# One encoder layer with 32 experts: token rows fetched from DRAM by indirect DMA in place of gather products, and 20 weight buffers in place of 16

## Chip, cores and metric

The kernel runs on one core of one Trainium2 chip. The metric is the device time of one execution in microseconds (us); lower is better. Engines are named as in the profile: PE is TensorE (PEld its weight loads), DVE VectorE, ACT ScalarE, POOL GpSimd, SP SyncE. SP, ACT and POOL each have an instruction queue from which they also start DMA transfers, one after another.

## What is computed

One layer on 512 tokens of width 1024, in float32. The attention half (three groups of heads, one input and one output projection, residual) is unchanged. The second half sends every token to 2 of 32 experts and adds the results to the residual:

```python
exp_idx = grp_idx[:, None] * EXPERTS_PER_GROUP + top_idx      # 2 experts per token
...
def expert_block(args):
    xb, e = args
    a = jax.nn.silu(xb @ w1[e]) * (xb @ w3[e])
    return a @ w2[e]
...
y = jnp.zeros((n + 1, d), h.dtype).at[row_tok].add(yb * row_gate[:, None].astype(h.dtype))
```

There are 512 x 2 = 1024 rows of tokens in all, spread over 32 experts. Every expert has w1 and w3 of 1024 x 512 and w2 of 512 x 1024, 6 MiB together. All 192 MiB of expert weights are read once.

## The kernel before

The program is a fixed order of instructions for every engine. It has three stages that matter here.

**Attention and projections** (up to about 364 us). `Group` objects load 1 MiB of w_in each, split it into a high and a low half and multiply; head units run beside them. Towards the end `wo_products` multiplies by w_out.

**Routing** (`route`, about 364 to 396 us). For each of four blocks of 128 tokens the kernel forms the normalised rows, the router's logits, the two experts and each row's place among that expert's rows. The order of its instructions comes from a small planner, `run_tasks`, with a duration for each task. Per block, ACT writes the rows in a rounded form `th` (`high`, L1141) and in full (`full`, L1146, two halves), and POOL subtracts them into the rest `tl` (`low`, L1151), so that `th + tl` is the row. `first_gather` (L1248) starts the gather for the first experts: a product of `th` and `tl` with a 0/1 matrix `G`, which picks tokens and turns them so that features lie on partitions.

**Experts** (from 396 us). Experts are worked in 16 pairs, expert pr and expert pr + 16 in the two halves of the array, 64 rows each. For a pair, `gate_half` and `hidden` multiply by w1 and w3 (`up_half`, L1398, tile h), turn the hidden rows (L1480, tile uTp), and `expert_out` multiplies by w2 (L1496, tile y). `combine` (L1416, L1417, tile c) adds the result to the tokens' rows with a 0/1 matrix `ot`; it is emitted inside the next pair's first product. `gather` (L1387, tile xTp) makes the next rows: two 16-product pieces per pair, each product 256 columns wide, for two pairs of experts at once, so every second pair finds its rows ready. `last_out` is the last pair, with its w2 cut into smaller pieces.

**Weights.** The 192 MiB come in 192 loads of 1 MiB, in the order in which they are used: four for w1, four for w3, four for w2 of each pair. (The last six are cut into smaller transfers.) `load_w` (L918) puts each on SP's queue. Load n goes to the buffer `RING[n % 16]`; a granule is a tile of 128 x 2048 float32, which one load fills. Several granules serve the attention stage first (b, q, h, g, m), others exist only once that stage's memory is free (d, e, j, k, v, w). Before the ninth load the ring is

```python
RING = "b q h h g g m m h h d e j k v w".split()
```

A transfer waits on SP until everything that reads the buffer's old content is done. All transfers behind it on SP's queue wait with it.

Of the kernel before, what the change touches and what calls it, by code (L numbers as in the profile page):

```python
# [23 lines left out]
P = 128  # L24
S = 512
# [10 lines left out]
RING = "b q h h g g m m h h d e j k v w".split()  # L36
# [8 lines left out]
def tile_encoder(ctx: ExitStack, tc, x, mem, g_mix, g_mem, g_ffk, w_in, w_kv, w_out, gains,  # L45
# [5 lines left out]
    gov = drp.tile([S, NE], F32, name="gov")  # L51
    man = ExitStack()
# [7 lines left out]
    BUFS = {"q": 1, "g": 2, "h": 4, "b": 1, "m": 2}  # L60
# [558 lines left out]
    def qk_tile(name, dt=F32):  # L619
        return big.tile([P, 2, S], dt, name=name, tag="qk", bufs=6)  # L620
# [11 lines left out]
    def qk(base, gi, order, rot, dd, key):  # L632
        def post(g, a, p):
            if key not in dd:
                dd[key] = qk_tile("qk")
# [33 lines left out]
    def na_v(n):  # L669
        def post(g, b, p):  # L670
            if "a" not in box_v:
                box_v["a"] = big.tile([P, 4, 512], F32, name="va", tag="va")
            return v_turn(g, b, p, "col", fac[:, 3, 0], box_v["a"][:, :, (2 * n + b) * P:(2 * n + b + 1) * P])
        return Group(w_in, VA + 256 * n, post, dims=True)
# [309 lines left out]
    load_w()  # L984
# [38 lines left out]
    at = small("at", [P, 4, 16])  # L1023
# [11 lines left out]
    def G_tile():  # L1035
        return rk.tile([P, 4, 2, P], F32R, name="G", tag="G")

    th, tl, Gs, first_x = [None] * 4, [None] * 4, [], []
# [48 lines left out]
    def route():  # L1087
# [12 lines left out]
        def rows(a):  # L1100
# [20 lines left out]
            for n in (1, 0):  # L1121
                t = task("P", 0.44, lambda n=n: turn_x(n), x_done.get((a, n)), *pt_free[-NPT:][:1] if len(pt_free) >= NPT else ())
                c = task("A", 0.48, lambda n=n: copy(n), t, rl_done.get(a - 2))
                pt_free.append(c)
                rl = task("P", 0.8, lambda n=n: logits_x(n), c, rl, free_lg.get(a - 2))
# [9 lines left out]
            def high():  # L1135
                if a < 3:
                    th[a], tl[a] = [qk_tile("th", F32R).rearrange("p a b -> p (a b)") for _ in range(2)]
                else:
                    t = big.tile([P, 4, 512], F32R, name="th3", tag="va")
                    th[a], tl[a] = t[:, 0:2].rearrange("p a b -> p (a b)"), t[:, 2:4].rearrange("p a b -> p (a b)")  # L1140
# [3 lines left out]
            def full(n):  # L1144
                st["f", n] = r2.tile([P, 2, 256], F32, name="xr", tag="pr", bufs=NPR).rearrange("p a b -> p (a b)")
                nc.scalar.activation(st["f", n].rearrange("p (k q) -> p q k", k=4),  # L1146
                                     x1[:, a].rearrange("p (q k) -> p q k", k=KT)[:, :, 4 * n:4 * n + 4], AF.Copy, scale=r)

            def low(n):
                c = slice(n * 512, (n + 1) * 512)  # L1150
                nc.gpsimd.tensor_sub(tl[a][:, c], st["f", n], th[a][:, c])  # L1151
            hi_done = task("A", 1.05, high, r_done)
            for n in range(2):
                f_done[a, n] = task("A", 0.62, lambda n=n: full(n), r_done, f_done.get((a - 2, n)))
                f_done[a, n] = task("G", 1.23, lambda n=n: low(n), hi_done, f_done[a, n])
            choose(a, lgt)

        def choose(a, lgt):
# [47 lines left out]
            t = v(0.1, lambda: V.tensor_add(at[:, a], d()[:, 0:16], d()[:, 16:32]), t)  # L1206

            for j in range(2):
                def slots(j=j):
                    if not Gs:  # L1210
                        Gs.append(G_tile())
                    V.tensor_scalar(Gs[0][:, a, j], places_, at[:, a, j:j + 1], None, op0=ALU.is_equal)
                G_last.append(v(0.2, slots, t))
# [25 lines left out]
            free_lg[a] = t[1]  # L1239
# [3 lines left out]
            def first_gather(i):  # L1243
                if a == 0:
                    first_x.append(bank("pj", 2, "xq"))
                for k in (2 * i, 2 * i + 1):
                    for n, t in enumerate((th[a], tl[a])):
                        nc.tensor.matmul(first_x[i][:, (k % 2) * 256:(k % 2) * 256 + 256], t[:, k * P:(k + 1) * P], Gs[0][:, a],  # L1248
                                         start=(a == 0 and k % 2 == 0 and n == 0), stop=(a == 3 and n == 1), skip_group_check=True)
            gt_ = None  # L1250
            for i in range(2):
                gt_ = task("P", 0.43, lambda i=i: first_gather(i), *G_last[-2:], f_done[a, 0], x_got.get((a - 1, i)), last_p[0], gt_)
                x_got[a, i] = gt_
# [9 lines left out]
        for a, n in LISTED:  # L1263
            block[0] = a

            def mm(a=a, n=n):
                wo_products(a, n, (0, 1, 2, 3))
                parts[a, n] = pos[n]
            p = task("P", 2.57, mm, *wop_prev[-2:-1], *last_p)
            last_p[:] = [p]  # L1270
            x_done[a, n] = task("V", 0.6, lambda a=a, n=n: add_x(a, n, parts[a, n]), p)
            wop_prev.append(x_done[a, n])
            sq_done[a, n] = task("A", 0.62, lambda a=a, n=n: square(a, n), x_done[a, n])
# [4 lines left out]
        task("P", 3.0, lambda: None, x_got[3, 1])  # L1278
# [31 lines left out]
    for n in range(2):  # L1310
        for a in range(4):
# [4 lines left out]
            def before():  # L1316
# [4 lines left out]
                if a == 0 and n == 1:  # L1321
                    load_w()
# [13 lines left out]
    load_w(2)  # L1336
# [11 lines left out]
    for tag, n, bufs in (("xT", 2, 6), ("u", 2, 1), ("uT", 2, 1), ("ringw", 8, 1), ("ringv", 8, 1)):  # L1348
        for _ in range(bufs):
            wk_.tile([P, n * 256], F32, name="place", tag=tag, bufs=bufs)  # L1350

    def scale_x(q, k0):
        xT = wk_.tile([P, 2, 2 * P], F32, name="xT", tag="xT", bufs=6)
        V.tensor_tensor(xT, q, gfk[:, 0, k0:k0 + 2].unsqueeze(2).to_broadcast([P, 2, 2 * P]), op=ALU.mult)  # L1354
        return xT

    xT = [scale_x(q.rearrange("p (k s) -> p k s", k=2), 2 * i) for i, q in enumerate(first_x)]
# [17 lines left out]
    def spread(pr):  # L1375

        G = G_tile()
        V.tensor_tensor(G, places_.unsqueeze(1).unsqueeze(1).to_broadcast([P, 4, 2, P]),
                        at[:, :, pr:pr + 2].unsqueeze(3).to_broadcast([P, 4, 2, P]), op=ALU.is_equal)
        return G  # L1380

    def gather(G, k0):
# [6 lines left out]
        return scale_x(q.rearrange("p (k j) s -> p k (j s)", j=2), k0)  # L1389
# [4 lines left out]
    def up_half(pr, w, q, p, between=()):  # L1394
        for k in range(4 * q, 4 * q + 4):
            for h in range(2):
                o = pr % 2 * P + h * 64
                nc.tensor.matmul(p[h * 64:(h + 1) * 64, :], xT[k // 2][:, k % 2, o:o + 64], wt[pr, w, q, h][:, k % 4, :],  # L1398
# [3 lines left out]
            if k % 4 == 1:  # L1402
                while between:
                    between.pop(0)()

    def up(pr, w, between=()):
        p, between = up_tile(w), list(between)
        for q in range(2):
            up_half(pr, w, q, p, between)
# [32 lines left out]
    G = Gs[0]  # L1442
    load_w(2)
    between, nxt = [], []
    p_first = []

    def gate_half(pr):
        nonlocal G, between
        if pr:
            p1 = up(pr, 0, between)  # L1450
        else:
# [4 lines left out]
            xT.extend([gather(G, k0) for k0 in (4, 6)])  # L1456
            up_half(0, 0, 1, p1)
        between = []
        u = wk_.tile([P, F], F32, name="u", tag="u", bufs=1)
        nc.scalar.activation(u, p1, AF.Silu)  # L1460
        if pr % 2 == 0 and pr + 2 < NPAIR:
            G = spread(pr + 2)
        return u

    def hidden(pr, u):

        nonlocal xT, nxt, between
        if pr:
            p3 = up(pr, 1, between)
# [3 lines left out]
        between = []  # L1473
        V.tensor_mul(u, u, p3)  # L1474
        rest = pr // 2 * 2 + 2 < NPAIR
        if rest:
            nxt.append(gather(G, pr % 2 * 4))
# [5 lines left out]
        if rest:  # L1483
            nxt.append(gather(G, pr % 2 * 4 + 2))
        if pr % 2:
            xT, nxt = nxt, []
# [19 lines left out]
    def last_out(pr, uT):  # L1506
# [13 lines left out]
        def gated(c0, n):  # L1520

            yh, yl = [wk_.tile([P, 512], F32R, name="y" + c, tag="xT", bufs=6)[:, 0:n] for c in "hl"]
# [20 lines left out]
        while between:  # L1543
            between.pop(0)()
# [30 lines left out]
    with tc.If(flag > 0):  # L1575
        with tc.tile_pool(name="ov", bufs=1) as ov, tc.tile_pool(name="ovps", bufs=1, space=PS) as ovs:
            with tc.For_i(0, NE) as e:
# [6 lines left out]
                for a in range(4):  # L1584
# [3 lines left out]
                    V.tensor_add(t, th[a], tl[a])  # L1588
# [3 lines left out]
                    for k in range(KT):  # L1592
                        q = ovs.tile([P, P], F32, name="ovq1")
                        nc.tensor.transpose(q, t[:, k * P:(k + 1) * P], ident)
# [89 lines left out]
```

## Time and profile before

| | us |
|---|---|
| median of 3 runs (874.48 to 875.97) | 874.78 |
| the profiled execution | 875.22 |
| its span | 873.4 |
| PE busy | 841.9 (96%) |
| DVE, ACT, POOL busy | 434.0, 267.1, 142.6 |

The profiled execution is 1.8 us longer than its span and 0.4 us longer than the median. The mean granted clock of TensorE is 0.98 of full. Matmuls overlap and their ends are modelled, so a busy share of 100% doesn't by itself say that PE is the limit; how often it waits, and for what, has to be read beside it. The second page section gives each engine's busy tenths in 40 slices, and the bytes moved in each; a slice in which the bytes per second stand at their highest and do not move is one in which the transfers run without a gap.

### The profile page before, as it was taken

How to read it: one execution, taken by the hardware profiler on the slowest of the kernel's cores; microseconds unless marked ns; L12 is line 12 of the kernel's file. 1: busy time of each engine (PE TensorE's matmuls, PEld its weight loads, DVE VectorE, ACT ScalarE, POOL GpSimd, SP SyncE). 2: the span in 40 equal slices, each digit the busy share in tenths (PEclk: the TensorE clock that was granted, in tenths of full speed). 3: DMA queues.
4: the chain of work that ended last, by engine and by line, in shares of the span. 5: the costliest groups of instructions: out<-in, count | busy, mean ns of one | idle time of the engine just before them, and what ended most of it. 6: DMA issues, size and time to landing. Idle time of an engine off the chain costs nothing.

```text
span 873.4 us, 13351 instructions
## 1 busy us (share of the span) xinstructions
PE 841.9 (96%) x5086; PEld 545.1 (62%) x5086; DVE 434.0 (50%) x1208; ACT 267.1 (31%) x776; POOL 142.6 (16%) x141
## 2 busy tenths in 40 slices
PE   7799999999899999989999999999999999999995
PEld 7789889879778767884545454545454545354333
DVE  6787796448759567482413241334133413341323
ACT  5667665665535544570010001000100010000001
POOL 5453222243322324160000000000000000000000
PEclk8999999999999999978999999999999999999998
DMA  9233113122122376848999999999999999999983
GB/s 314 73 97 105 50 51 96 49 74 92 49 78 62 101 216 231 328 146 318 375 421 422 419 421 421 421 421 421 421 421 421 421 421 421 422 421 420 421 298 99
DMA packets 63475, 237.53 MB, mean 272 GB/s; under 512 B 8240, under 2 KB 32816, under 8 KB 39600
## 3 DMA queue, kind: packets, MB, share of 16 engines
q1 hardware_dynamic: 55376, 230.18, 66.7%
q10 hardware_dynamic: 8032, 6.45, 3.0%
q8 instruction: 42, 0.69, 0.3%
q14 instruction: 25, 0.20, 0.1%
HBM read 234.45 MB, written 2.16 MB: 271 GB/s over the span
## 4 chain that ended last, share of the span: by engine, by line
PE 77%; DVE 12%; ACT 3%; DMA 3%; issue 3%; POOL 1%; ACTq 0%; DVEq 0%; SPq 0%; POOLq 0%
PE h L1398 26%; PE y L1496 12%; PE xTp L1387 7%; PE pj L231 4%; PE c L1416 4%; PE pj L232 3%; PE pj L233 3%; PE c L1417 3%; PE pj L241 1%; DMA nab<-in_na_tab_dram 1%; PE pj L243 1%; PE pj L242 1%; PE acc L392 1%; PE lg L348 1%; DVE rw L282 1%
## 5 line engine op out<-in xcount | busy, mean ns | idle before, releaser
L1398 PE MATMUL h<-w,xT 128*64 128x512 f32 x1024 | 227.2, 596 | 0.0
L1398 PEld LDWEIGHTS h<-w,xT 128*64 128x64 f32 x1024 | 72.0, 137 | 141.7 <-issue 139.0
L1496 PE MATMUL y<-w,uT 128*64 128x512 f32 x480 | 106.3, 595 | 0.0
L188 POOL TENSOR_TENSOR wp<-wc,wp 128x512 fp32r<-128x512 f32 x51 | 66.9, 1315 | 129.6 <-ACT wp L187 109.4
L1474 DVE TENSOR_TENSOR u<-u,h 128x512 f32<-128x512 f32 x16 | 11.0, 688 | 150.1 <-PE h L1398 150.1
L231 PE MATMUL pj<-wp,hTh 128*128 128x256 f32 (+1 forms) x268 | 79.3, 296 | 1.9 <-ACT hTh L768 1.0
L1419 DVE TENSOR_TENSOR x<-x,c 128x512 f32<-128x512 f32 x120 | 73.1, 682 | 12.3 <-PE c L1417 12.3
L232 PE MATMUL pj<-wp,hTh 128*128 128x256 f32 (+1 forms) x268 | 76.7, 286 | 1.3 <-POOL wp L188 1.3
L233 PE MATMUL pj<-wp,hTl 128*128 128x256 f32 (+1 forms) x268 | 76.5, 285 | 0.2 <-DVE hTl L771 0.2
L1496 PEld LDWEIGHTS y<-w,uT 128*64 128x64 f32 x480 | 33.2, 137 | 62.5 <-issue 59.4
L1502 DVE SCALAR_TENSOR_TENSOR yl<-y,gate,yh 128x512 fp32r<-128x512 f32 x30 | 22.5, 751 | 94.5 <-ACT yh L1501 94.5
L1387 PEld LDWEIGHTS xTp<-G,th 128*128 128x128 f32 x480 | 59.3, 189 | 12.2 <-issue 12.2
L1387 PE MATMUL xTp<-G,th 128*128 128x256 f32 x480 | 64.9, 287 | 0.0
L1460 ACT ACTIVATE u<-h 128x512 f32<-128x512 f32 x16 | 9.6, 597 | 149.6 <-PE h L1398 149.6
L1501 ACT ACTIVATE yh<-y,gate 128x512 fp32r<-128x512 f32 x30 | 20.6, 687 | 112.6 <-PE y L1496 111.6
L231 PEld LDWEIGHTS pj<-wp,hTh 128*128 128x128 f32 (+1 forms) x268 | 51.6, 192 | 4.9 <-issue 1.4
L232 PEld LDWEIGHTS pj<-wp,hTh 128*128 128x128 f32 (+1 forms) x268 | 51.6, 193 | 1.7 <-POOL wp L188 1.7
L1482 ACT ACTIVATE uT<-uTp 128x512 f32<-128x512 f32 x16 | 9.6, 597 | 139.3 <-PE uTp L1480 139.3
L233 PEld LDWEIGHTS pj<-wp,hTl 128*128 128x128 f32 (+1 forms) x268 | 51.6, 192 | 0.4 <-DVE hTl L771 0.4
L1416 PE MATMUL c<-yh,ot 128*128 128x512 f32 x120 | 48.7, 406 | 0.0
L1417 PE MATMUL c<-yl,ot 128*128 128x512 f32 x120 | 47.0, 392 | 0.0
L1354 DVE TENSOR_TENSOR xT<-xTp,gfk 128x512 f32<-128x512 f32 x30 | 20.8, 692 | 52.5 <-PE xTp L1387 52.5
(315 smaller groups left out, 1481.1 us busy)
## 6 DMA issues: line engine op xcount, KB each, us to landing
w<-in_w_dram SPq DMA_DIRECT2D x188, 1024.0 KB, 13.1
wc<-in_w_in_dram SPq DMA_DIRECT2D x15, 1024.0 KB, 5.5
wo<-in_w_out_dram SPq DMA_DIRECT2D x4, 1024.0 KB, 5.1
w<-in_w_dram SPq DMA_DIRECT2D x6, 512.0 KB, 15.0
wc<-in_w_kv_dram SPq DMA_DIRECT2D x2, 1024.0 KB, 8.3
x<-in_x_dram ACTq DMA_DIRECT2D x4, 512.0 KB, 9.4
nab<-in_na_tab_dram ACTq DMA_DIRECT2D x8, 248.0 KB, 2.8
x_sb<-in_x_dram SPq DMA_DIRECT2D x3, 512.0 KB, 6.2
```

What stands on the lines that cost most here:

```text
L188: (eng or nc.gpsimd).tensor_sub(dst[1], src, dst[0])
L231: nc.tensor.matmul(o, th, self.hi[k], start=(k == 0), stop=False)
L232: nc.tensor.matmul(o, th, self.lo[k], start=False, stop=False)
L233: nc.tensor.matmul(o, tl, self.hi[k], start=False, stop=(k == KT - 1))
L1354: V.tensor_tensor(xT, q, gfk[:, 0, k0:k0 + 2].unsqueeze(2).to_broadcast([P, 2, 2 * P]), op=ALU.mult)
L1387: nc.tensor.matmul(q[:, 2 * (k - k0):2 * (k - k0) + 2, :], t[a][:, k * P:(k + 1) * P], G[:, a], start=(n == 0), stop=(n == 7))
L1398: nc.tensor.matmul(p[h * 64:(h + 1) * 64, :], xT[k // 2][:, k % 2, o:o + 64], wt[pr, w, q, h][:, k % 4, :], start=(k == 0), stop=(k == KT ...
L1416: nc.tensor.matmul(c, ot[:, a], yh, start=True, stop=False)
L1417: nc.tensor.matmul(c, ot[:, a], yl, start=False, stop=True)
L1419: V.tensor_add(sl, sl, c)
L1496: nc.tensor.matmul(y[h * 64:(h + 1) * 64, :], uT[:, f, h * 64:(h + 1) * 64], rows_of(wt[pr, 2, q, h])[:, f % 2, n * 512:(n + 1) * 512], st ...
L1502: V.scalar_tensor_tensor(yl, y, gate[:, pr:pr + 1], yh, op0=ALU.mult, op1=ALU.subtract)
```

## The change

1. Each block's normalised rows are written once in full (`full`), to the granules k0 (blocks 0 and 1) and va (blocks 2 and 3), and stored to a DRAM tensor `xd` by ACT's queue (4 transfers of 512 KiB). The rounded rows, the rest and POOL's subtractions go.
2. The first pair's rows are still made by products, now in float32 from the full rows, 128 columns wide: 16 in `first_gather` for half the features, 16 in `gather_first` for the other half, after the first pair's first two half products.
3. For the 15 other pairs, POOL issues one indirect DMA each: 128 places of one row of 4 KiB, by an index list `where_`; a place without a row has an index out of range and is left alone. PE turns the rows (`turn_rows`, 8 transposes per pair). Two buffers take turns, and a fetch goes out when the buffer's rows have been turned.
4. `combine` of a pair now stands in the next pair's `hidden`, between the transposes and the product with w2.
5. A query tile and its key tile share a granule (k0, k1, k2), and with va these four become weight buffers: the ring has 20. The first load moves behind the last load of w_out; four loads are emitted at once there, four one step later, four more after `route`.

```diff
-RING = "b q h h g g m m h h d e j k v w".split()
+RING = "k2 b q k1 h h g g k0 va m m h h d e j k v w".split()
...
-                nc.scalar.activation(th[a].rearrange("p (k q) -> p q k", k=KT), x1[:, a].rearrange("p (q k) -> p q k", k=KT),
-                                     AF.Copy, scale=r)
...
-                nc.gpsimd.tensor_sub(tl[a][:, c], st["f", n], th[a][:, c])
...
+            def full():
+                if a % 2 == 0:
+                    xr2.append(granule(("k0", "va")[a // 2], "xr"))
+                xr.append(xr2[a // 2][:, 2 * (a % 2):2 * (a % 2) + 2].rearrange("p a b -> p (a b)"))
+                nc.scalar.activation(xr[a], x1[:, a], AF.Copy, scale=r)
+
+            def store():
+                nc.scalar.dma_start(xd[a * P:(a + 1) * P], xr[a])
...
-                if a == 0 and n == 1:
-                    load_w()
+                if a == 2 and n == 1:
+                    load_w(4)
                 if a == 3 and n == 1:
                     load_w(4)
...
     route()
-    load_w(2)
+    load_w(4)
...
+    def rows_load(pr):
+        if pr < NPAIR:
+            nc.gpsimd.indirect_dma_start(out=rows_in[pr % 2], out_offset=None, in_=xd,
+                                         in_offset=bass.IndirectOffsetOnAxis(ap=where_[:, pr:pr + 1], axis=0),
+                                         bounds_check=S - 1, oob_is_err=False)
...
+    def gather_first():
 
         q = trp("xTp")
-        for k in (k0, k0 + 1):
-            for n, (t, a) in enumerate((t, a) for a in range(4) for t in (th, tl)):
-                nc.tensor.matmul(q[:, 2 * (k - k0):2 * (k - k0) + 2, :], t[a][:, k * P:(k + 1) * P], G[:, a],
-                                 start=(n == 0), stop=(n == 7))
...
+        for k in range(4, KT):
+            for a in range(4):
+                nc.tensor.matmul(q[:, k - 4], xr[a][:, k::KT], Gs[0][:, a], start=(k == 4 and a == 0), stop=(a == 3), skip_group_check=True)
+        return scale_x(q, 1)
+
+    def turn_rows(pr):
+        nxt = []
+        for half in range(2):
+            q = trp("xTp")
+            for k in range(4):
+                nc.tensor.transpose(q[:, k], rows_in[pr % 2][:, 4 * half + k::KT], ident)
+            nxt.append(scale_x(q, half))
+        rows_load(pr + 2)
+        return nxt
```

The weight transfers on SP's queue around the ninth one. A name is w, which weight (0 is w1, 1 is w3, 2 is w2), expert, half, a running number; in brackets stand the semaphores that the transfer, or a wait just ahead of it, waits for. Before:

```order
L938 DMA w0_0_1_4481<-in_w1_dram 128x2048 [waits DMAHW5_49,Pool_49]
L938 DMA w0_16_1_4483<-in_w1_dram 128x2048 [waits DMAHW6_49,Pool_49]
L938 DMA w1_0_1_5041<-in_w3_dram 128x2048 [waits DMAHW7_49,DVE_49]
L938 DMA w1_16_1_5043<-in_w3_dram 128x2048 [waits DMAHW0_49]
L940 DMA w2_0_0_5053<-in_w2_dram 128x2048 [waits DMAHW1_49,PE_49]
L940 DMA w2_16_0_5055<-in_w2_dram 128x2048 [waits DMAHW2_49,PE_49]
L940 DMA w2_0_1_5057<-in_w2_dram 128x2048 [waits DMAHW3_49,DVE_49,PE_49]
L940 DMA w2_16_1_5059<-in_w2_dram 128x2048 [waits DMAHW4_49,DVE_49,PE_49]
```

And now:

```order
L946 DMA w0_16_1_4479<-in_w1_dram 128x2048 [waits DMAHW6_49]
L946 DMA w1_0_1_4481<-in_w3_dram 128x2048 [waits DMAHW7_49,Pool_49]
L946 DMA w1_16_1_4483<-in_w3_dram 128x2048 [waits DMAHW0_49,Pool_49]
L948 DMA w2_0_0_4995<-in_w2_dram 128x2048 [waits DMAHW2_49,DMAHW1_49,DMAHW5_49,PE_49,Activation_49]
L948 DMA w2_16_0_4997<-in_w2_dram 128x2048 [waits DMAHW4_49,DMAHW3_49,DMAHW6_49,PE_49,Activation_49]
L948 DMA w2_0_1_4999<-in_w2_dram 128x2048 [waits DMAHW7_49]
L948 DMA w2_16_1_5001<-in_w2_dram 128x2048 [waits DMAHW0_49]
L946 DMA w0_1_0_5011<-in_w1_dram 128x2048
L946 DMA w0_17_0_5013<-in_w1_dram 128x2048
```

The ninth and tenth transfers (w2 of experts 0 and 16, first halves) now go to k0 and va, which hold the full rows of tokens, and wait for ACT, for the stores to xd and for PE's last reading of those rows; the ones after them wait for little of their own.

PE at the end of `hidden` of an early pair, from the last product with w3 to the first with w2. Before (pair 0):

```order
L1398 MATMUL h_5097<-w_16_1_5043,xT 64x512
L1387 MATMUL xTp<-G,th 128x256 x6
L1387 MATMUL xTp<-G,th_4936 128x256 x2
L1387 MATMUL xTp<-G,th 128x256 x6
L1387 MATMUL xTp<-G,th_4936 128x256 x2
L1480 MATMUL uTp<-ident,u 128x128 x4
L1387 MATMUL xTp<-G,th 128x256 x6
L1387 MATMUL xTp<-G,th_4936 128x256 x2
L1387 MATMUL xTp<-G,th 128x256 x6
L1387 MATMUL xTp<-G,th_4936 128x256 x2
L1496 MATMUL y<-w_0_0_5053,uT 64x512
```

And now (pair 1):

```order
L1408 MATMUL h_5235<-w_17_1_5079,xT 64x512
L1397 MATMUL xTp<-ident,rows 128x128 x8
L1480 MATMUL uTp<-ident,u 128x128 x4
L1423 MATMUL c<-yh,ot 128x512
L1424 MATMUL c<-yl,ot 128x512
```

The 32 gather products of a pair became 8 transposes, and the 16 products of `combine` (the last two rows, eight times) stand ahead of y.

## Rows read from the trace of the kernel before

**Rows 1.** page, the span in 40 slices of 21.8 us: PE busy tenths, GB/s moved:

```profile
PE   7799999999899999989999999999999999999995
...
GB/s 314 73 97 105 50 51 96 49 74 92 49 78 62 101 216 231 328 146 318 375 421 422 419 421 421 421 421 421 421 421 421 421 421 421 422 421 420 421 298 99
```

**Rows 2.** busy time by window: PE, PEld, DVE, ACT, POOL, PEclk, DMA share, GB/s:

```profile
385.00:390.00 5.00, 4.49 (x25) 4.28 (x25) 3.82 (x26) 4.20 (x6) 2.68 (x7) 0.50 0.00 2
390.00:395.00 5.00, 3.73 (x21) 3.55 (x22) 4.38 (x29) 0.60 (x3) 2.44 (x3) 0.50 0.00 0
500.00:550.00 50.00, 50.00 (x260) 25.20 (x258) 17.64 (x27) 4.54 (x7) 0.00 (x0) 1.00 1.01 421
844.00:847.00 3.00, 3.00 (x14) 2.08 (x14) 3.00 (x6) 0.00 (x0) 0.00 (x0) 1.00 0.84 270
847.00:850.00 3.00, 3.00 (x16) 1.01 (x14) 1.41 (x3) 0.00 (x0) 0.00 (x0) 1.00 0.21 67
850.00:853.00 3.00, 2.21 (x11) 0.65 (x8) 0.96 (x2) 0.00 (x0) 0.00 (x0) 1.00 0.00 0
```

**Rows 3.** timeline of SP's transfers: start us, us they spread over, line, tiles, count:

```profile
326.46 20.25 SPq L938 DMA_DIRECT2D w<-in_w_dram  x7
360.64 10.34 SPq L940 DMA_DIRECT2D w<-in_w_dram  x4
376.26 28.79 SPq L938 DMA_DIRECT2D w<-in_w_dram  x8
```

**Rows 4.** the same for one pair of experts and the next:

```profile
500.07 4.24 SPq L940 DMA_DIRECT2D w<-in_w_dram  x4
...
529.35 4.24 SPq L940 DMA_DIRECT2D w<-in_w_dram  x4
```

**Rows 5.** DMA issues by line: tiles, queue, count, KB each, us to landing:

```profile
w<-in_w_dram SPq DMA_DIRECT2D x188, 1024.0 KB, 13.1
```

**Rows 6.** instructions on tile w, last line: issue to landing:

```profile
DMA to landing us min/median/max: 4.9/13.2/19.8
```

**Rows 7.** who waited for whom, 380 to 873 us: us in total, times, longest:

```profile
PEld h L1398 <- DMA w<-in_w_dram: 2.0, 7, 0.3
```

**Rows 8.** timeline of PE inside one pair: start us, us, line, tiles, count:

```profile
503.41 2.18 PE L1387 MATMUL xTp<-G,th 128*128 128x256 f32 x16
505.42 0.65 PE L1480 MATMUL uTp<-ident,u 128*128 128x128 f32 x4
505.83 2.17 PE L1387 MATMUL xTp<-G,th 128*128 128x256 f32 x16
```

**Rows 9.** chain that ended last, through routing: start us, us, engine tile line:

```profile
369.16 2.13 ACT th L1141
371.29 0.94 ACT xr L1146
...
373.25 1.10 ACT xr L1146
...
388.61 1.22 DVE G L1212
...
396.15 7.88 PE h L1398 x32
404.02 4.02 PE xTp L1387 x32
```

**Rows 10.** timeline of POOL in routing, one of eight such rows:

```profile
388.46 1.28 POOL L1151 TENSOR_TENSOR th<-xr,th 128x512 fp32r<-128x512 f32 x1 [0.38 <-ACT xr L1146]
```

**Rows 11.** chain that ended last, at the end of the span:

```profile
843.73 0.23 PE c L1417
...
854.27 6.24 PE y L1516 x40
...
861.64 1.01 PE y L1516 x8
```

More of the change, by code (lines that the diff above doesn't have):

```diff
@@ L1022, in tile_encoder @@
     gt = small("gt", [P, 2, 4])
[L1023 removed]
+    at = small("at", [P, 4])
     nc.gpsimd.iota(iota, pattern=[[1, P]], base=1, channel_multiplier=0, allow_small_or_imprecise_dtypes=True)
@@ L1133, in rows @@
             lgt = task("V", 0.17, lambda: V.scalar_tensor_tensor(lg[:, a], st["l"][:, 0:36], r, br, op0=ALU.mult, op1=ALU.add), rl, r_done)
[L1135 to L1140, printed above, removed]
-                nc.scalar.activation(th[a].rearrange("p (k q) -> p q k", k=KT), x1[:, a].rearrange("p (q k) -> p q k", k=KT),
-                                     AF.Copy, scale=r)
[L1144 to L1150, printed above, removed]
-                nc.gpsimd.tensor_sub(tl[a][:, c], st["f", n], th[a][:, c])
[L1152 to L1155, printed above, removed]
+            def full():
[5 more added lines that the diff above has]
+                nc.scalar.dma_start(xd[a * P:(a + 1) * P], xr[a])
+            f_done[a] = task("A", 1.1, full, r_done, f_done.get(a - 1))
+            task("A", 0.4, store, f_done[a])
             choose(a, lgt)
@@ L1205, in choose, with slots @@
             t = v(0.14, lambda: V.tensor_mul(d(), mb[:, a], st["q"]), mb_done[a], rk_)
[L1206 to L1213, printed above, removed]
+            t = v(0.1, lambda: V.tensor_add(at[:, a:a + 1], d()[:, 0:1], d()[:, 16:17]), t)
+            def slots():
+                if not Gs:
+                    Gs.append(G_tile())
+                V.tensor_scalar(Gs[0][:, a], places_, at[:, a:a + 1], None, op0=ALU.is_equal)
+            G_last.append(v(0.2, slots, t))
             ge_ = v(0.07, lambda: V.tensor_scalar(ge(), G4, m(0), None, op0=ALU.subtract), t0)
@@ L1401, in up_half, with up @@
                 load_w(2)
[L1402 to L1407, printed above, removed]
+    def up(pr, w):
+        p = up_tile(w)
         for q in range(2):
-            up_half(pr, w, q, p, between)
+            up_half(pr, w, q, p)
         return p
@@ L1455, in gate_half @@
             up_half(0, 1, 0, p_first[0])
-            xT.extend([gather(G, k0) for k0 in (4, 6)])
+            xT.append(gather_first())
             up_half(0, 0, 1, p1)
-        between = []
         u = wk_.tile([P, F], F32, name="u", tag="u", bufs=1)
         nc.scalar.activation(u, p1, AF.Silu)
-        if pr % 2 == 0 and pr + 2 < NPAIR:
-            G = spread(pr + 2)
         return u
     def hidden(pr, u):
-        nonlocal xT, nxt, between
+        nonlocal xT
         if pr:
-            p3 = up(pr, 1, between)
+            p3 = up(pr, 1)
         else:
@@ L1472, in hidden @@
             up_half(0, 1, 1, p3)
-        between = []
         V.tensor_mul(u, u, p3)
-        rest = pr // 2 * 2 + 2 < NPAIR
-        if rest:
-            nxt.append(gather(G, pr % 2 * 4))
+        if pr + 1 < NPAIR:
+            xT = turn_rows(pr + 1)
         t = trp("uTp")
@@ L1482, in hidden @@
         nc.scalar.activation(uT, t, AF.Copy)
[L1483 to L1486, printed above, removed]
+        while between:
+            between.pop(0)()
         return uT
```

97 lines of the change are left out of this document (48 added, 49 removed).

## The prediction, made before the changed kernel ran

> **What bounds the kernel now.** I read the page's 40 slices first, to see where transfers and PE are full. From slice 20 (about 436 us) to slice 36 the bytes stand at 421 GB/s with hardly a change, and PE's digit is 9 [rows 1]. Two resources look full at once, so the next question is which waits for which. In a window of that stage the DMA share is 1.01 [rows 2]: transfers run without a gap. SP's timeline gives PE's pace, since a transfer leaves when PE frees a buffer: the four w2 transfers of one pair and of the next stand 29.28 us apart [rows 4]. The transfers' own pace is 12 loads x 1.0486 MB / 421 GB/s = 29.9 us a pair. PE is thus 0.6 us a pair faster than the weights and lives from a lead that it gathered earlier. The waits confirm it: in the whole stage PE's products with w1 and w3 waited for weights 7 times, 2.0 us in all [rows 7]. Before, PE is the bound, and the weights are 2% short of being one. Any time taken from PE in this stage must come up against them.
>
> So what matters is when the stream of weights starts, what it carries, and what follows its end. Before, SP had issued eight weight transfers by 347 us, four more by 371, and the next eight from 376 us on [rows 3]; nothing moves from 385 to 395 us [rows 2]. The stream ends at about 848 us: from 847 to 850 only 67 GB/s move, after that none [rows 2]. The last products with w2 start at 854.27 us, 19.1 us before the span's end, and their last piece at 861.64, 11.8 us before it [rows 11].
>
> **The change part by part.**
>
> *Gather products out, transposes in.* A pair loses 32 products: from 503.41 and 505.83 us to the next work some 2.0 + 2.1 = 4.1 us [rows 8]. It gains 8 float32 transposes; four such take from 505.42 to 505.83, 0.4 us [rows 8], so 0.8 us. PE needs 29.3 - 4.1 + 0.8 = 26.0 us a pair. The weights still need 29.9. The other 3.9 us a pair turn into waiting for weights. By itself this part moves the end only through the lead that PE had.
>
> *The ninth transfer.* This decides. The ring now begins k2 b q k1 h h g g, then k0 and va. The first eight go out as their buffers come free, as before about 326 to 347 us. But k0 and va hold the full rows, and these are read last by `gather_first`, which stands in the expert stage behind the first two half products. The ninth transfer waits for it at the head of SP's queue, and 183 loads stand behind it. In the trace before, 20 loads had been issued by 405 us (8, 4 and 8 [rows 3]). Now it is 8. Four more buffers don't help, since nothing can be put into them.
>
> When is `gather_first` done? Before, the expert stage starts at 396.15 us [rows 9]. On the chain through routing stand ACT's writes of th and xr: 2.13 + 0.94 + 1.10 = 4.2 us a block, on the chain for two blocks [rows 9]. One full write of 1024 columns replaces them, about the two halves' rows together less their strided output (1.1 to 2.0 us), and a store's issue. That is 2 to 2.6 us a block, 4 to 5 us if all of it was the limit. Four vector instructions in routing last 1.0 to 1.5 us beside a subtraction on POOL, such as the 1.22 us for G beside POOL's 1.28 us [rows 9, 10]; these subtractions go, 2 us on the last block's chain. PE has its own work there at half clock (granted 0.50, busy 3.7 to 4.5 of 5 us [rows 2]). Bounds for the start are 396 (nothing gained) and 387 us; I take 390, two thirds of it, since several engines are near their limits. Then 7.9 us of first half products [rows 9] and `gather_first`: 16 products in float32 of 128 columns, by the transposes 16 x 0.1 = 1.6 us at least [rows 8], by the 32 wider products that it replaces 4.0 us at most [rows 9]; I take 3.7, near the latter, because a product in float32 moves more than a transpose. The ninth transfer goes out at 390 + 7.9 + 3.7 + 0.4 for SP = 402 us (398 to 408).
>
> *The stream.* A transfer on a free queue lands 4.9 us after its issue [rows 6], 2.5 of them its own bytes, so 2.4 us of start. Then 184 loads of 1024 KB [rows 5], 1.0486 MB each, / 421 GB/s = 458.3 us. The final small pieces run slower (270 GB/s in 844 to 847 [rows 2]): 1.5 us.
>
> *The indirect fetches.* Of the 1024 rows some 15/16 are fetched, 4 KiB each: 3.9 MB. The trace has no transfer that is issued by POOL. The stage has no free share of the transfers (1.01 [rows 2]), so the lower bound, nothing, holds only if the fetches fall into holes of the stream; at the stream's rate they cost 9.3 us; if their rows load the 16 engines unevenly, so that the stream waits for the fullest, twice that, 18.6. I take 9.3: that share row is the nearest. A rule of the Trainium skill speaks to this point ("DMA: Bandwidth & Descriptors", Issuing engines are not separate DMA queues): transfers started from SP, ACT or GpSimd end up on the same 16 engines and interleave. By that rule the fetches would cost 9.3 us, by separate queues nothing, and the sum would be 882; no run so far shows POOL's. POOL has no other work in the stage (0.00 busy [rows 2]), so nobody is queued behind its wait for PE. The rows are fetched almost a pair ahead, so PE should not wait for them. xd's 2 MiB are written while nothing moves [rows 2]: 0.
>
> *`combine` moved, and the tail.* Its 16 products of 0.23 us [rows 11] now stand after the last weights with w1 and w3, ahead of the last products with w2: 3.7 us later in the last pair. In other pairs they fill time in which PE would wait. PE no longer lags behind the stream at the end, so between the stream's end and the span's end lie less than the 25.4 us of before (848 to 873.4). If only the last piece of w2 is left then, 11.8 us; if all of the last pair's w2 is, 19.1. w3 lands four loads, 10 us, before the end; 2 us of products, 2 us for the hidden rows and 3.7 of `combine` put the start of y some 3 us before the end, so 19.1 - 3 = 16 us.
>
> **Sum.** 402 + 2.4 + 458.3 + 9.3 + 1.5 = 873.5 us for the stream's end, against 848; 873.5 + 16 = 889.5 us of span; with the 1.8 us that lie around it 891.3. That is 16 us over the profiled execution of 875.22, and over the median of 874.78 (the runs spread by 1.5 us) 1.9%.
>
> **Rivals.**
>
> *Fetches weigh double* (uneven engines, 18.6 us): 901 us. For it: a row of tokens fills only about half of a pair's 128 places. Against it: rows land in runs that may be spread well. The Trainium skill has a mechanism that would act the same way ("DMA: Bandwidth & Descriptors", Latency and other measured facts): engines 7 and 15 are usually the slower ones, with descriptors written by GpSimd as a guess at the cause.
>
> *Early and light*: routing gains its full 9 us (gather done at 399), fetches fall into holes (0), 12 us of tail: 399 + 2.4 + 458.3 + 0 + 1.5 + 12 + 1.8 = 875, no change. All three have to come true.
>
> *The gate doesn't hold*, the case on the other side: the ninth transfer leaves at about 361 us, as before, since its buffer is read no later than in routing. The place is SP's queue ahead of the ninth load. Then the stream ends about 848 + 9.3 for the fetches - 10 for the stretch from 385 to 395 us that the extra buffers fill = 847 us, and 847 + 16 + 1.8 = 865 us, faster by 1.1%. It decides in proportion: every us by which the ninth transfer leaves earlier takes one off, and the break-even is 402 - 16.5, about 385 us.
>
> *The clock falls.* In routing it is granted at half, 1.2 instead of 2.4 GHz, while PE has small products and waits [rows 2]. If waiting for weights did the same for whole pairs, 26 us would become up to 52 a pair and PE the bound: 390 + 16 x 52 = 1222 us at worst, and 402 + 12 x 29.9 + 4 x 52 = 969 if four pairs ran so. Against it: from 850 to 853 us PE is busy 2.21 of 3 us, about as much as it would be now, and keeps the full clock [rows 2].
>
> **How the numbers follow.** Forecast 892 us: 0.76 (its own range 882 to 898). Fetches double: 0.10. Early and light: 0.05, split between no change and slightly slower. Gate doesn't hold: 0.05. Clock: 0.04. For 8 in 10, take the forecast's bounds and the double fetches: 880 to 905; what lies below and above is some 0.1 each. About 0.2%, 1.7 us, is what a measurement of this kernel can tell from no change. Faster 0.05; same 0.03; slower 0.92.
>
> **What would show each step.** In the trace after: the ninth weight transfer on SP issued at 398 to 408 us and not earlier, with almost no bytes between about 365 us and then but for xd's stores; 421 GB/s from there to about 873 us; PE waiting for weights several us in every pair, in waits of up to some 2 us; the expert stage starting near 390 us, with no long vector instructions in routing; 16 us from the stream's end to the span's end. The prediction is wrong if the ninth transfer leaves before 385 us, if the rate per load changes, or if PE waits for rows and not for weights.

## The result, and the profile after

The changed kernel takes 897.7 us (median, 897.4 to 899.5) beside 874.6 for the kernel before: ratio 1.0265, interval 1.0247 to 1.0283. It is slower by 2.6%, 23 us, and 5.7 us beyond the 892 that was forecast. The profiled execution has a span of 896.1 us.

The page's slices of the changed kernel (22.4 us each), to be held against [rows 1]:

```profile
PE   8799999999899999989898889889988998899996
...
PEclk8999999999999999979999999999999999999998
...
GB/s 326 51 94 102 52 91 50 48 115 48 95 44 92 133 227 304 72 50 244 423 403 427 426 425 425 427 426 426 427 426 426 425 426 426 426 427 426 426 407 155
```

In the slices that begin at 358 and 381 us next to nothing moves: 72 and 50 GB/s. From the slice at 426 us on the stream stands at 423 to 427 GB/s, but for one slice of 403 and its end; before, it stood at some 421. PE, full before, now has eights in that stage.

SP's timeline shows why (start, duration, line, what, count; in a group, the time from its first to its last):

```profile
326.62 20.81 SPq L946 DMA_DIRECT2D w<-in_w_dram  x8
411.09 2.29 SPq L948 DMA_DIRECT2D w<-in_w_dram  x4
413.43 12.79 SPq L946 DMA_DIRECT2D w<-in_w_dram  x8
429.03 19.61 SPq L948 DMA_DIRECT2D w<-in_w_dram  x4
```

Eight weight transfers leave by 347 us, as before (seven of them in [rows 3], after one at 305.63). The ninth leaves at 411.09; before, it left at 360.64 and twenty had left by 405. The windows (busy time of PE, PEld, DVE, ACT, POOL with counts, then clock, DMA share, GB/s) show the empty stretch and the full stage behind it:

```profile
360.00:380.00 20.00, 19.73 (x122) 17.45 (x120) 10.94 (x63) 11.83 (x33) 2.96 (x9) 1.00 0.20 79
380.00:390.00 10.00, 9.22 (x72) 9.03 (x71) 7.69 (x48) 2.92 (x10) 6.04 (x15) 0.93 0.13 53
390.00:400.00 10.00, 7.58 (x26) 4.01 (x27) 4.55 (x31) 1.48 (x2) 2.65 (x3) 0.56 0.12 32
400.00:410.00 10.00, 10.00 (x45) 7.06 (x41) 0.00 (x0) 0.00 (x0) 0.00 (x0) 1.00 0.09 27
410.00:420.00 10.00, 9.22 (x37) 4.09 (x38) 0.69 (x1) 0.60 (x1) 0.00 (x0) 0.83 0.79 304
...
500.00:550.00 50.00, 45.02 (x206) 19.44 (x204) 16.23 (x26) 3.76 (x6) 1.98 (x2) 1.00 1.01 426
```

On PE's timeline stand, in this order, the first half products, `gather_first` (L1389) and the second half products. The transfer leaves towards the end of the second row:

```profile
395.29 8.85 PE L1408 MATMUL h<-w,xT 128*64 128x512 f32 x32 [0.53 <-DVE xT L1345]
404.07 7.89 PE L1389 MATMUL xTp<-G,xr 128*128 128x128 f32 x32
412.74 8.66 PE L1408 MATMUL h<-w,xT 128*64 128x512 f32 x32 [0.78 <-DVE xT L1345]
```

The waits from 380 us to the end (total, times, longest) answer to [rows 7]; 7 waits and 2.0 us have become 48 and 79.3 on the weight-load side, the same stalls seen from the products being the second row:

```profile
PEld h L1408 <- DMA w<-in_w_dram: 79.3, 48, 2.3
PE h L1408 <- DMA w<-in_w_dram: 40.2, 37, 1.4
```

### The profile page after: what moved, and what is told of

The parts are those of the page before. It is cut to its first block, busy times and chain, and to the rows that moved or that the text cites. A ratio compares the mean times of both kernels' runs of the same rounds, so it can differ in the third digit from the quotient of the medians.

```text
span 896.1 us, 12694 instructions
## 1 busy us (share of the span) xinstructions
PE 823.3 (92%) x4758; PEld 517.8 (58%) x4758; DVE 421.1 (47%) x1200; ACT 256.6 (29%) x768; POOL 149.9 (17%) x150
## 5 line engine op out<-in xcount | busy, mean ns | idle before, releaser
L1408 PE MATMUL h<-w,xT 128*64 128x512 f32 x1024 | 248.2, 604 | 41.7 <-DMA w<-in_w_dram 40.2
L1408 PEld LDWEIGHTS h<-w,xT 128*64 128x64 f32 x1024 | 81.7, 138 | 203.1 <-issue 115.2
L232 PE MATMUL pj<-wp,hTh 128*128 128x256 f32 (+1 forms) x268 | 79.3, 296 | 0.7 <-ACT hTh L776 0.7
L1361 POOL DMA_INDIRECT rows<-xd,where x15 | 15.1, 1009 | 381.0 <-PE uTp L1480 235.7
L232 PE MATMUL pj<-wq,hTh 128*128 128x256 f32 (+1 forms) x124 | 37.4, 301 | 2.8 <-ACT raw L279 2.8
L234 PE MATMUL pj<-wq,hTl 128*128 128x256 f32 (+1 forms) x124 | 35.6, 287 | 0.0
## 6 DMA issues: line engine op xcount, KB each, us to landing
w<-in_w_dram SPq DMA_DIRECT2D x188, 1024.0 KB, 19.6
```

What stands on the lines that cost most here:

```text
L232: nc.tensor.matmul(o, th, self.hi[k], start=(k == 0), stop=False)
L234: nc.tensor.matmul(o, tl, self.hi[k], start=False, stop=(k == KT - 1))
L1361: nc.gpsimd.indirect_dma_start(out=rows_in[pr % 2], out_offset=None, in_=xd, in_offset=bass.IndirectOffsetOnAxis(ap=where_[:, pr:pr + 1], ...
L1408: nc.tensor.matmul(p[h * 64:(h + 1) * 64, :], xT[k // 4][:, k % 4, h * 64:(h + 1) * 64], wt[pr, w, q, h][:, k % 4, :], start=(k == 0), sto ...
```

## Experiments

### Is it the held transfer? k0 and va out of the list

```diff
-RING = "k2 b q k1 h h g g k0 va m m h h d e j k v w".split()
+RING = "k2 b q k1 h h g g m m h h d e j k v w".split()
```

> The changed kernel, but k0 and va are taken out of the list of buffers, which is then k2 b q k1 h h g g m m h h d e j k v w: 18 buffers, none of which holds the full rows. Theory (the gate on k0 and va costs the time): the ninth weight transfer leaves at about 347 us instead of 411, eighteen loads have landed by about 404, and 26 of them by 430, against some 15 in the changed kernel; 11 loads x 2.46 us = 28 us come off: 870 us (864 to 874), faster than the kernel before by about 0.5%. Rival (the stream's own rate with the fetches in it, or the fetches themselves, make it slow): the end hardly moves, 890 us or more.

Measured: 867.6 us (867.1 to 868.3), ratio 0.9909 (0.9888 to 0.9930). With two buffers fewer the kernel is 30 us faster than the changed one, and faster than the one before. SP's timeline and the slices of this version (21.6 us each):

```profile
323.70 20.50 SPq L946 DMA_DIRECT2D w<-in_w_dram  x8
344.29 15.60 SPq L948 DMA_DIRECT2D w<-in_w_dram  x4
362.29 36.11 SPq L946 DMA_DIRECT2D w<-in_w_dram  x8
401.03 14.67 SPq L948 DMA_DIRECT2D w<-in_w_dram  x4
GB/s 324 66 98 106 50 55 95 49 72 96 49 79 62 90 182 293 424 236 318 308 424 426 426 425 424 427 425 427 426 427 425 427 426 426 426 426 428 425 400 136
```

The ninth transfer leaves at 344.29 us, twenty have left by 398.4, and the empty slices hold 424 and 236 GB/s. The stage behind them runs at the same 426 GB/s as in the changed kernel, so the rival (a slow stream) is out. The hold on SP's queue costs more than the whole loss: without it the rest of the change is a gain of 8 us.

### What is the shorter pair on TensorE worth?

First the list of the kernel before, with the new fetch; then 24 needless transposes a pair in the 18-buffer version.

```diff
+RING = "b q h h g g m m h h d e j k v w".split()
     route()
-    load_w(4)
+    load_w(2)
```

> The changed kernel with the list of buffers of the kernel before (b q h h g g m m h h d e j k v w): 16 buffers, the new fetch. Theory (a buffer that is loaded ahead is worth its load, TensorE's shorter pair is worth nothing by itself): two loads fewer ahead than with k2 and k1, 2 x 2.46 = 5 us more than 867.6, so 872.5 (870 to 876), within a few us of the kernel before. Rival (the shorter pair is what makes the 18 buffer version faster): 868 as there.

Measured: 872.2 us (870.2 to 873.5), ratio 0.9959 (0.9940 to 0.9978). With as many buffers as before, all the rest of the change together (fetch and transposes in place of the gather products, shorter routing writes, `combine` moved) is worth 3 us; the two further buffers are worth 4.5 (5 expected).

```diff
-            for k in range(4):
+            for k in (0, 1, 2, 3) * 4:
                 nc.tensor.transpose(q[:, k], rows_in[pr % 2][:, 4 * half + k::KT], ident)
```

> The version without k0 and va in the list, with every transpose of a fetched row tile done four times (24 more on TensorE in a pair, 0.12 to 0.15 us each, some 3 us a pair; the results are the same). Theory (weights bound the stage: 30.3 us for the twelve loads and the fetch of a pair, against 26 us of TensorE's work): the extra work goes into the waits for weights, 867.6 to 871 us. Rival (TensorE sets the pace, so removing its gather products was worth their time): 15 x 3 = 45 us more, 912.

Measured: 874.5 us (872.8 to 878.0), ratio 0.9991 (0.9973 to 1.0009). SP's groups show TensorE's pace in the early pairs, while buffers are loaded far ahead. In the 18-buffer version, and then with the extra transposes, from one transfer group to its like a pair later:

```profile
462.11 4.24 SPq L948 DMA_DIRECT2D w<-in_w_dram  x4
488.15 7.64 SPq L948 DMA_DIRECT2D w<-in_w_dram  x4
```
```profile
469.88 4.24 SPq L948 DMA_DIRECT2D w<-in_w_dram  x4
498.55 4.24 SPq L948 DMA_DIRECT2D w<-in_w_dram  x4
```

A pair takes 26.0 us (462.11 to 488.15) and 28.7 (469.88 to 498.55): some 2.6 us more, 40 us over 15 pairs. The time rose by 6.9, so five sixths went into waits for weights, but not all: I had set the limit at 871. The waits for weights, the first weight transfers and the last group of six show where the rest went. The 18-buffer version, and then with the extra work:

```profile
PEld h L1408 <- DMA w<-in_w_dram: 42.2, 30, 2.2
830.97 11.76 SPq L954 DMA_DIRECT2D w<-in_w_dram  x6
```
```profile
PEld h L1408 <- DMA w<-in_w_dram: 1.1, 4, 0.3
326.82 20.67 SPq L946 DMA_DIRECT2D w<-in_w_dram  x8
835.08 11.76 SPq L954 DMA_DIRECT2D w<-in_w_dram  x6
```

With the extra work TensorE hardly waits any more, but the stream is only 1.0 us longer: 508.3 us from the first transfer to the last group, beside 507.3 (from 323.70 to 830.97). The profiled spans differ by 10.4 us, 3.1 of them ahead of the first transfer; the rest of the loss lies behind the stream: from the last group to the span's end there are 41.0 us (of 876.1) instead of 34.7 (of 865.7), since TensorE comes late to the last products with w2. They start 19.5 us behind the last group (at 854.59), and not 14.7 (845.62).

### Does the end follow the held transfer?

`gather_first` goes ahead of the first half products; nothing else changes.

```diff
+            xT.append(gather_first())
             up_half(0, 0, 0, p1)
             up_half(0, 1, 0, p_first[0])
-            xT.append(gather_first())
```

> The changed kernel with gather_first ahead of the first two half products, not behind them; the same work on PE. Theory (the end follows the ninth transfer one to one): it leaves at 395 + 7.9 + 0.4 = 403 us instead of 411, so 8 us come off, 889.5 us, less up to 3 us if the stream runs dry near 430 to 440 us, where the next buffers come free only when PE has finished the first pair, which this edit doesn't move: 889 to 893 us. Rival (the ninth transfer isn't what sets the end): 897 us, no change.

Measured: 888.3 us (887.2 to 889.7), ratio 1.0146 (1.0123 to 1.0168): 9.4 us less. In its profile the ninth transfer leaves at 399.95 us, 11.1 before the 411.09 of the changed kernel (2.2 of which lie in front of all weights: the first one leaves at 324.45 instead of 326.62). The span ends 10.0 us earlier (886.1 against 896.1): the end follows it nearly one to one, and the feared dry stretch at 430 to 440 us did not come (423 GB/s there).

Next, k0 and va at the end of the list, loaded behind `gather_first`:

```diff
+RING = "k2 b q k1 h h g g m m h h d e j k v w k0 va".split()
-            if k % 4 == 3:
+            if k % 4 == 3 and (pr or q):
                 load_w(2)
     ...
             xT.append(gather_first())
+            load_w(4)
```

> The changed kernel with k0 and va moved to the end of the list of buffers (..., v w k0 va), and the loads into them and those behind them recorded after gather_first. Theory (what costs is the number of loads that stand behind the held one, and how long the transfers then lack work): loads 0 to 17 leave early, the nineteenth is held until gather_first ends at about 409 us. The stream lacks work from about 397 to 411 us; by 430 us some 25 loads have landed against 27 without k0 and va in the list: 2 x 2.46 = 5 us more than that version's 867.6, so 872 us (869 to 876), near the kernel before. Rival (any hold of SP's queue behind gather_first costs as in the changed kernel): 890 or more; other rival (two more buffers pay for themselves): 865 or less.

Measured: 872.1 us (871.6 to 872.5), ratio 0.9959 (0.9937 to 0.9980). The hold is still there, and its window is as empty as any:

```profile
405.00:410.00 5.00, 5.00 (x22) 5.00 (x23) 0.00 (x0) 0.00 (x0) 0.00 (x0) 1.00 0.00 0
```

But eighteen loads stand ahead of it instead of eight. So 20 buffers with the hold late are 4.5 us slower than 18 without it and 25.6 faster than 20 with it early: the price is the time for which transfers lack work.

Then both edits together, the loads into k0 and va recorded right behind `gather_first`:

```diff
+            xT.append(gather_first())
+            load_w(2)
             up_half(0, 0, 0, p1)
             up_half(0, 1, 0, p_first[0])
-            xT.append(gather_first())
-            load_w(4)
+            load_w(2)
```

> The same order of buffers (..., v w k0 va), and gather_first ahead of the first half products, the loads into k0 and va recorded behind it. Theory: the held load leaves at about 401 us, when the stream has just run dry, and from then on it is not short of work again, where the version without k0 and va was at 410 to 420 us (146 GB/s); by 430 us nearly 29 loads have landed against 27: some 4 us less than 867.6, so 864 us (861 to 867). Rival (the first pair's products, 8 us later, free their buffers 8 us later and take the gain back): 868 or more.

Measured: 864.3 us (861.8 to 867.0), ratio 0.9871 (0.9837 to 0.9905). From 410 to 415 us, where the 18-buffer version has 7 GB/s (first row), this one has 431 (second):

```profile
410.00:415.00 5.00, 5.00 (x18) 1.41 (x16) 0.00 (x0) 0.05 (x1) 0.00 (x0) 0.71 0.02 7
```
```profile
410.00:415.00 5.00, 5.00 (x29) 2.34 (x26) 1.12 (x2) 0.60 (x1) 0.00 (x0) 1.00 1.02 431
```

### What do the fetches cost?

First 13 of the 15 fetches are left out, and later pairs reuse the rows that lie in the two buffers; then every fetch is made twice.

```diff
-        rows_load(pr + 2)
         return nxt
```

> The changed kernel without 13 of the 15 fetches: those of pairs 1 and 2 stay, later pairs reuse the rows that lie there, so part of the computation is left out. Fetches that cost nothing: 897.7 us. Fetches at the rate of the stream (3.96 MB / 15 / 0.421 = 0.63 us each): 13 x 0.63 = 8 us less, 889.5. In the trace of the changed kernel twelve loads take 30.3 us on average while fetches run and 29.4 in the last two pairs, which have none: 0.95 us each would give 12 us less, 885.5. Twice the bytes' time: 16 us less, 881.5.

Measured: 886.8 us (884.9 to 888.1), ratio 1.0126 (1.0102 to 1.0150): 10.9 us less.

```diff
-        if pr < NPAIR:
+        for _ in range(2 if pr < NPAIR else 0):
             nc.gpsimd.indirect_dma_start(...)
```

> The changed kernel with each indirect fetch issued twice, the same rows into the same tile. Fetches that cost nothing: 897.7 us. At the bytes' rate: 15 x 0.63 = 9.4 us more, 907. At the 0.95 us that the periods of twelve loads show: 14 us more, 912. At twice the bytes' time: 916.5. PE should still not wait for rows, only for weights.

Measured: 909.2 us (908.2 to 910.7), ratio 1.0385 (1.0362 to 1.0408): 11.6 us more.

The traces price it more finely, by the time from the ninth transfer to the last group of six. Changed kernel, without the 13, and with all twice:

```profile
411.09 2.29 SPq L948 DMA_DIRECT2D w<-in_w_dram  x4
...
861.87 11.76 SPq L954 DMA_DIRECT2D w<-in_w_dram  x6
```
```profile
410.19 2.48 SPq L948 DMA_DIRECT2D w<-in_w_dram  x4
...
467.74 17.39 SPq L946 DMA_DIRECT2D w<-in_w_dram  x8
...
763.44 17.56 SPq L946 DMA_DIRECT2D w<-in_w_dram  x8
...
852.28 11.93 SPq L954 DMA_DIRECT2D w<-in_w_dram  x6
```
```profile
411.57 2.50 SPq L948 DMA_DIRECT2D w<-in_w_dram  x4
...
874.62 11.76 SPq L954 DMA_DIRECT2D w<-in_w_dram  x6
```

That is 450.8, 442.1 and 463.1 us. Two of the 15 fetches leave at 396.6 and 398.1 us, while next to nothing else moves, so 13 stand beside the stream. One of these costs (450.8 - 442.1) / 13 = 0.67 us, a second one of the same rows 12.3 / 13 = 0.94, against 0.63 for its bytes at 421 GB/s. The whole times give 10.9 / 13 = 0.84 and 11.6 / 13 = 0.89. A fetch is thus neither free nor of double price. Why a second one costs more was not tried. Without fetches a pair's twelve loads take 29.57 us on average (ten pairs, 467.74 to 763.44); the changed kernel takes 30.34 for the like (469.52 to 772.90), 0.77 more. The 0.95 us that I had read off the last two pairs of the changed kernel is above all three figures for a first fetch.

### Why did routing hardly get shorter?

The gather products of routing are left out for three of the four row blocks, in the 18-buffer version.

```diff
-                for k in range(4):
+                for k in range(4) if a == 3 else ():
                     nc.tensor.matmul(first_x[0][:, k * P:(k + 1) * P], xr[a][:, k::KT], Gs[0][:, a],
-                                     start=(a == 0 and k == 0), stop=(a == 3), skip_group_check=True)
+                                     start=(k == 0), stop=True, skip_group_check=True)
```

> The version without k0 and va in the list, with routing's gather products (xq, float32, four a row block) left out for the first three of four row blocks, so part of the computation is left out. Theory (in routing TensorE had become the limit: its four groups of xq last 2.2 us each): the expert stage starts up to 3 x 2.2 = 6.6 us earlier, at 386 to 389 us on the scale on which it starts at 392.1, so 63 to 66 us behind the leaving of the third weight transfer instead of 67.3. Rival (the decisions on VectorE are the limit, and xq lies beside them): it starts within 1 us of where it did. The end moves by less, 862 to 868 us, because the stream sets it.

Measured: 865.7 us (863.7 to 868.1), ratio 0.9891 (0.9859 to 0.9922). The first weight transfer leaves at 326.41 us and the expert stage starts at 392.56, 66.2 us later; with the products it is 392.07 - 323.70 = 68.4 (68.3 to 68.7 in seven versions that have them). Of the 6.6 us left out, 2.2 came back. TensorE then waits longer in routing, for VectorE and GpSimd (waits from 380 us; the 18-buffer version waits 1.0 us for O and not for `val`):

```profile
PE rk L1197 <- DVE O L1188: 1.5, 1, 1.5
PE tb L1250 <- POOL val L1235: 1.4, 2, 1.2
```

Neither case held by itself: TensorE's products and the decisions are within about 2 us of each other.

### A version without the fault

If the first pair's second half is fetched too, `gather_first` goes, and the full rows are last read in routing.

```diff
+RING = "k2 b q k1 h h g g m m h h d e j k v w k0 va".split()
-        for k in range(4, KT):
-            for a in range(4):
-                nc.tensor.matmul(q[:, k - 4], xr[a][:, k::KT], Gs[0][:, a], ...)
+        for k in range(4):
+            nc.tensor.transpose(q[:, k], rows_in[0][:, 4 + k::KT], ident)
+        rows_load(2)
     ...
-    for pr in (1, 2):
+    for pr in (0, 1):
         rows_load(pr)
```

> The changed kernel with the second half of the first pair's rows taken by an indirect fetch and four transposes, as for the other pairs, so that gather_first's 16 products go; the list of buffers is ..., v w k0 va, with nothing recorded later. Theory (the fault is that a load stands behind the last reader of the full rows): k0 and va are free when routing's own products and the stores end, all 20 loads have left by about 392 us, TensorE's first pair is 6 us shorter, and the stream does not run dry after 390 us, where with gather_first ahead it lost some 4 us between 395 and 410 us; one fetch more, 0.7: 861 us (858 to 864). Rival (the first fetch lands late behind the weights, TensorE waits for it at 401 us for 5 us or more, and buffers come free no earlier): 865 to 868.

Measured: 863.2 us (860.5 to 864.4), ratio 0.9868 (0.9845 to 0.9891). Twenty loads have left by 393.6 us. It cannot be told from the version with the early `gather_first`, and two spots may have taken back some of the 3 us that were forecast beyond it: TensorE starts the second half at 404.67, 2.4 us behind the first one's end, and at 435 to 445 us the stream is short.

The second spot has a cause that SP's waits and ScalarE's timeline give away: one load, and ScalarE's write of uT, wait for the small store `gov`.

```profile
SPq L948 <- DMA gov<-wkb: 13.2, 1, 13.2
438.22 0.60 ACT L1482 ACTIVATE uT<-uTp 128x512 f32<-128x512 f32 x1 [9.51 <-DMA gov<-wkb]
```

The store's source `wkb` lies in the buffer of uT; TensorE waited 0.9 us for that write.

```diff
-        nc.scalar.dma_start(gov.rearrange("(a p) e -> p a e", p=P), wkb[:, 0])
+        nc.gpsimd.dma_start(gov.rearrange("(a p) e -> p a e", p=P), wkb[:, 0])
```

> The version whose first pair is fetched too, with the small store gov issued by GpSimd instead of ScalarE. In the trace of that version the 36th weight transfer leaves 13.6 us behind the one ahead of it (424.6 to 438.2 us), because it waits for the semaphore that gov's store signals, and that store lands late behind the queued weights; from 435 to 440 us 332 GB/s move, from 440 to 445 us 397. Theory (that wait is what leaves the stream short): 426 GB/s in those windows, the gap between the two transfers under 4 us, 1.5 us less in all: 861.7 us (860 to 863.2). Rival (the stream is short there for another reason, or the store now holds up GpSimd's next fetch): 863 us or more.

Measured: 862.1 us (860.2 to 862.4), ratio 0.9860 (0.9836 to 0.9884), the fastest version here; 1.4% ahead of the kernel before, though its 1.2 us over the last one is inside both spreads. The trace is plainer: both waits are gone. How much each of the two cost by itself was not tried. With `gov` on ScalarE, then on GpSimd: SP's group, the window, and the store's time to landing:

```profile
424.62 14.83 SPq L948 DMA_DIRECT2D w<-in_w_dram  x4
435.00:440.00 5.00, 4.07 (x23) 3.28 (x24) 4.14 (x7) 0.60 (x1) 0.99 (x1) 1.00 0.92 332
DMA to landing us min/median/max: 13.8/13.8/13.8
```
```profile
424.11 4.24 SPq L948 DMA_DIRECT2D w<-in_w_dram  x4
435.00:440.00 5.00, 5.00 (x27) 3.89 (x27) 4.89 (x9) 0.60 (x1) 1.03 (x1) 1.00 1.00 423
DMA to landing us min/median/max: 6.4/6.4/6.4
```

## Why the prediction came out as it did

The sign, the range and the mechanism were right. The sum was 6.6 us short of the span (889.5 against 896.1), the difference of larger errors.

**The gate.** Right: SP's queue stood behind the last reader of k0 and va, and nothing moved meanwhile. Taking the two buffers out of the list gives the rival's other world: its working said 865, measured 867.6. That these are so close is partly luck, since the working had the ninth transfer at 361 us and 20 buffers, and the run 344 us and 18.

**The time of the ninth transfer.** The step that failed: 402 forecast (398 to 408), 411.09 measured, 9 us, in three parts. The expert stage started at 395.29, not 390: beside [rows 9] (396.15) routing gained about 1 us where I had 6 (1.5 from the first product with w_out that both traces show, at 325.40 and 326.05 us). The lower bound of 387 was too low as well: its own terms, 4 to 5 us and 2, add up to 7 and not to 9. I had priced the writes and the subtractions that went away by what they last on the chain, though products and decisions were as near to the limit. The version that leaves routing's products out shows the pair of them: it takes away 6.6 us and gets 2.2. The first half products took 8.8 us instead of 7.9, part of them at half clock (granted 0.56 in 390 to 400 us). And `gather_first` lasted 7.9 us, 7.0 of them until the ninth transfer left, where I took 3.7 out of 1.6 to 4.0. My upper bound was the 32 wider products that it replaces; but those were in another number format, and a product in float32 stands in the trace as two records of 0.25 us (32 in 7.89). The changed code gave the format away, and a bound from products of another format was none.

**The stream.** 184 loads at 421 GB/s were to take 458.3 us. At 29.57 us for twelve they take 453.4, 4.9 less. The 421 of [rows 2] was right for the kernel before; that it would hold for the changed one was my assumption, and the list of signs named it. The fetches cost 13 x 0.67 = 8.7 us (10.9 by the whole times; 9.3 forecast). In the other direction, one dry spot at 448 to 452 us cost some 1.2; ahead of it SP had waited 14.5 us for the store `gov`:

```profile
446.00:448.00 2.00, 2.00 (x12) 0.58 (x9) 0.00 (x0) 0.00 (x0) 0.00 (x0) 1.00 1.01 424
448.00:450.00 2.00, 2.00 (x13) 1.17 (x11) 0.85 (x2) 0.00 (x0) 0.00 (x0) 1.00 0.78 213
450.00:452.00 2.00, 2.00 (x13) 1.74 (x12) 1.89 (x4) 0.60 (x1) 0.99 (x1) 1.00 0.93 385
```

So 411.1 + 2.4 + 453.4 + 8.7 + 1.2 + 1.5 = 878.3 us for the stream's end, and the windows have it at about 877.5:

```profile
876.00:877.00 1.00, 1.00 (x5) 0.37 (x5) 1.00 (x2) 0.00 (x0) 0.00 (x0) 1.00 0.76 266
877.00:878.00 1.00, 1.00 (x8) 0.42 (x6) 1.00 (x3) 0.00 (x0) 0.00 (x0) 1.00 0.49 174
```

**The fetches.** The middle of the three prices was the right one: 8.7 to 10.9 us measured for 9.3. The rival of double weight is out: 18.6 us were its price. The rule of the Trainium skill that was weighed ("DMA: Bandwidth & Descriptors", Issuing engines are not separate DMA queues) agrees with a price of 0.67 to 0.84 us a fetch beside 0.63 for its bytes. What the same page says of two slower engines (Latency and other measured facts) no run here shows: none looks at single DMA engines.

**The pair on TensorE.** 26.0 us forecast; 26.0 measured in the 18-buffer version, from 462.11 to 488.15. That it would turn into waits was right: 3 us for the whole part in the version with the old list, and those include a shorter tail. One step of the prediction does not follow from its own figures: it calls the weights 2% short of being the bound, but its 29.9 us for a pair's loads are more than TensorE's 29.3. TensorE hardly waited then because of the lead, and not because it was the slower of the two.

**The tail.** 16 us forecast, 896.1 - 877.5 = 18.6 measured. The last products with w2 start at 876.52, 1 us ahead of the stream's end and not 3 (by the prediction's own terms, 10 - 2 - 2 - 3.7, it was 2.3):

```profile
876.52 1.94 PE L1514 MATMUL y<-w,uT 128*64 128x512 f32 x8
```

From there to the end is 19.6 us, as in [rows 11] (19.1).

**The clock.** The rival fell: with TensorE waiting in every pair the granted clock stayed at 1.00 (2.4 GHz) in 500 to 550 us, at 45.0 busy of 50.

In all: +9.1 for the ninth transfer, -4.9 for the weights, -0.6 for the fetches, +1.2 for the dry spot, +2.6 for the tail: +7.4, where the span gives +6.6. The 9 us of the failed step would have been the miss by themselves; that the total came out nearer was luck.

## What to carry to other kernels

A buffer lent out of a ring has a date of return: find its last reader in the order of the program, and count the loads that stand behind its own in the queue. What it costs is the time for which transfers then lack work. A place at the end of the ring made 2.6% slower into 0.4% faster, an earlier last reader alone into 1.5% slower, and both together into 1.3% faster. And time taken from an engine beside a full stream was worth little here: the whole rest of the change gave 3 us, though TensorE had 3.3 us less to do in each of 15 pairs. So start the stream earlier first.

## What the runs showed of the hardware

- A store of 64 KB, issued while weight loads were queued, landed after 13.8 us from ScalarE's queue and after 6.4 from GpSimd's; in the kernel before, from ScalarE's queue, after 6.3. By the semaphores in the profile a later load on SP waited for the first of these. It has no need of the store's data: with the store on GpSimd that load had left by 428.4 us, before the store landed (424.2 + 6.4).
- GpSimd needed 1.0 us for each indirect fetch; from its issue to its landing the median was 8.0 us, beside 20 us for a weight load in the same stage.
- From 500 to 550 us every version with the fetch moved 425 or 426 GB/s, the one without most fetches 427, and the kernel before 421. Neither the list of 16 buffers nor TensorE's fuller time brings the 421 back (425 and 426). What in the old gather slowed the transfers was not tried.
